# Seven half-size products for 16 up pairs, and the first FFN in blocks

## The chip, the cores and the metric

One core of a Trainium2 chip runs the program. The metric is device time in microseconds, the median of the runs. A core has TensorE (PE in the rows; PEld is its weight load), VectorE (DVE), ScalarE (ACT), GpSimd (POOL), and SyncE (SP), which only issues transfers here. Each engine works through its own queue in the order that was fixed when the program was built.

## The reference

A trunk of two layers over 512 positions with 1024 channels, float32. Each layer is a token mixer (gated linear attention, then a short gated convolution) and a causal ConvFFN, each behind an RMSNorm and with a residual addition; a last RMSNorm ends it. The change touches the first ConvFFN only:

```python
def conv_ffn(h, w_up, conv_w, w_down):
    up = causal_dwconv(h @ w_up, conv_w)      # depthwise, 3 taps over positions
    a, u = up[..., :D_FF], up[..., D_FF:]     # D_FF = 2816
    return (jax.nn.silu(a) * u) @ w_down
```

## The kernel before, in words

Activations stand transposed: `x[k]` is a tile of 128 channels by 512 positions, eight of them. Every float32 operand of a large product is split into a rounded part h and a rest l (both in the type fp32r), and a product is three matmuls, wh xh + wh xl + wl xh (`mm3`, L181). ScalarE makes h by a copy, VectorE makes l by a subtraction (L110, L111 for weights; L201, L202 for activations).

Weights come in units of 128 x 1024 (eight blocks of 128 x 128). `Weights.load` issues a unit's transfer on SP's queue into one of four raw tiles (`wraw`), `Weights.part` splits it into one of three pairs of tiles (`wsp`), and `Weights.take`, called before each group of matmuls, loads one unit further, splits the unit two ahead and gives out the current one. `group` (L188) takes a unit and runs its 24 matmuls of 512 columns into one of eight PSUM banks.

`ffn_up` (L487) runs over 22 pairs: the group of 128 gate channels, the group of 128 value channels; then the after-work: VectorE scales both by the inverse norm r (L499) into tiles u (three buffers), ScalarE and VectorE form the convolution (L245 to L247), ScalarE takes silu (L501), VectorE multiplies (L502), and the product is split into g{j}h and g{j}l (`split_to`). All 22 split products are held. Then the down stage: `residual` (L472) takes for each of eight blocks of channels one group of 66 matmuls over three units, adds it to x, and prepares the next norm (`norm_parts`, `norm_squares`).

The build has a planner that interleaves the queues: an instruction can stand before one that is earlier in the source when the planner finds it ready first; the silu, for example, stands ahead of the second convolution. The last row block of the second FFN is computed in two halves of 256 positions (`last_group`, L541), whose matmuls have 256 columns and a weight load each.

Of the kernel before, what the change touches and what calls it, by code (L numbers as in the profile page):

```python
# [10 lines left out]
F32 = mybir.dt.float32  # L11
F32R = mybir.dt.float32r
AF = mybir.ActivationFunctionType
ALU = mybir.AluOpType
# [14 lines left out]
DOWN_CUTS = ((0, 8), (8, 16), (16, 22))  # L29


@with_exitstack
def trunk_kernel(ctx, tc, xT, w_qk, w_v, w_g, w_up_gate, b_gate, w_go, w_sc, w_so, w_up, w_dn,
# [44 lines left out]
    class Weights:  # L78
        def __init__(self):
            self.units, self.raw, self.split, self.hold = [], {}, {}, {}  # L80
            self.nl = self.ns = self.ng = 0

        def load(self, between=lambda: None):
            if self.nl < len(self.units):
                src = self.units[self.nl]
                r = wraw.tile([P, UNIT], F32, tag="wraw", name=f"wr{self.nl}")
                n = src.shape[1]
                step = (UNIT // 4, UNIT // 2, UNIT)[min(self.nl, 2)]
                for c in range(0, n, step):
                    nc.sync.dma_start(r[:, c:min(c + step, n)], src[:, c:min(c + step, n)])  # L90
                    between()
                self.raw[self.nl] = r[:, :n]
                self.nl += 1

        def part(self):
            if self.ns < len(self.units):
                tiles = self.hold.pop(self.ns, lambda: None)()
                r = self.raw.pop(self.ns)
# [3 lines left out]
                if not tiles:  # L102
                    h = wsp.tile([P, UNIT], F32R, tag="wh", name=f"wh{self.ns}")
                    l = wsp.tile([P, UNIT], F32R, tag="wl", name=f"wl{self.ns}")
                blocks = []
                for i, c in enumerate(range(0, n, step)):
# [3 lines left out]
                    S.copy(hh, r[:, c:e])  # L110
                    V.tensor_sub(ll, r[:, c:e], hh.bitcast(F32))  # L111
# [4 lines left out]
        def take(self):  # L116

            self.load()
# [5 lines left out]
    W.units += [w_qk[i] for i in range(8)] + [w_v[i] for i in range(8)] + [w_g[i] for i in range(8)]  # L124
    W.units += [w_go[i] for i in range(8)]

    def ff_units(l):
        u = [w_up[l, j] for j in range(2 * NFF)]
        return u + [w_dn[l, m][:, a * P:b * P] for m in range(KD) for a, b in DOWN_CUTS]

    W.units += ff_units(0) + [w_sc[i] for i in range(3 * KD)] + [w_so[i] for i in range(KD)] + ff_units(1)
# [374 lines left out]
    gp = ffn_up(0)  # L506
    residual(lambda m: group(f"dn{m}", gp, nunits=3), 2)
# [31 lines left out]
    HT = T // 2  # L539
# [123 lines left out]
```

## Time and profile before

| | us |
|---|---|
| median of 3 runs (1117.83 to 1118.11) | 1117.9 |
| the profiled execution | 1117.47 |
| its span | 1115.8 |
| TensorE busy | 1106.3 |
| VectorE busy | 682.1 |
| ScalarE busy | 461.0 |
| POOL busy | 5.0 |

A busy share is a mean over stages with different limits. TensorE's matmuls overlap (each row's duration is longer than the step to the next), so a step is read from a stretch divided by its count, not from a mean duration. Transfers: 108.14 MB, 97 GB/s; nearly all on SP's queue, none issued by POOL.

### The profile page before, as it was taken

Reading aid. Unit: us, or ns where it says so; the run is one execution under the profiler, and the core shown is the slowest. Engines: PE = TensorE matmul, PEld = TensorE weight load, DVE = VectorE, ACT = ScalarE, POOL = GpSimd, SP = SyncE. Lnnn points to the kernel's source line nnn. Section 1 sums busy time; section 2 is a strip of 40 time slices with the busy share of each in tenths; the row PEclk is TensorE's granted clock in tenths of the full one; section 3 lists DMA queues with packets and bytes.
Section 4 is the critical chain, followed back from the end, with each engine's and each line's share of the span. In section 5 each row is a group of like instructions: output and inputs, shape, how many; then the busy total and the mean of one; then the engine's idle time right before and its main releaser. Section 6 shows DMA issues by size and latency. Waiting matters only on the chain.

```text
span 1115.8 us, 12505 instructions
## 1 busy us (share of the span) xinstructions
PE 1106.3 (99%) x5020; PEld 920.9 (83%) x5020; DVE 682.1 (61%) x854; ACT 461.0 (41%) x610; POOL 5.0 (0%) x18
## 2 busy tenths in 40 slices
PE   9999999999999999999999999999999999999997
PEld 7888888888888888888888888888888888888887
DVE  7864675597777777433336555558777777753232
ACT  6565664354444444332332222334444444432241
POOL 1000000000000000000000000000000000000000
PEclk9999999999999999999999999999999999999999
DMA  7231213222233222233232222222323222232312
GB/s 258 77 104 66 75 58 114 95 95 95 95 100 103 100 95 90 86 104 104 90 111 95 95 95 95 95 95 95 102 104 96 95 95 95 90 103 86 102 55 76
DMA packets 33182, 108.14 MB, mean 97 GB/s; under 512 B 3618, under 2 KB 6434, under 8 KB 33124
## 3 DMA queue, kind: packets, MB, share of 16 engines
q1 hardware_dynamic: 33124, 107.34, 29.5%
q8 instruction: 39, 0.64, 0.2%
q14 instruction: 19, 0.16, 0.0%
HBM read 105.23 MB, written 2.10 MB: 96 GB/s over the span
## 4 chain that ended last, share of the span: by engine, by line
PE 99%; DMA 0%; DVE 0%; ACT 0%; SPq 0%; issue 0%; DVEq 0%
PE up L186 43%; PE dn L186 20%; PE g L186 4%; PE v L186 4%; PE scb L186 4%; PE scu L186 4%; PE scc L186 4%; PE go L186 4%; PE so L186 4%; PE k L186 2%; PE q L186 2%; PE dn7b L186 1%; PE dn7a L186 1%; PE o L407 1%; PE o L409 0%; DMA x<-in_xT 0%
## 5 line engine op out<-in xcount | busy, mean ns | idle before, releaser
L110 ACT CAST wh<-wr 128x1024 fp32r<-128x1024 f32 (+3 forms) x201 | 204.8, 1019 | 370.8 <-PE dn L186 113.1
L111 DVE TENSOR_TENSOR wl<-wr,wh 128x1024 fp32r<-128x1024 f32 (+3 forms) x201 | 237.7, 1183 | 154.6 <-ACT wh L110 152.2
L186 PE MATMUL up<-xh,wh 128*128 128x512 f32 x704 | 273.9, 389 | 0.0
L186 PE MATMUL up<-xl,wh 128*128 128x512 f32 x704 | 273.9, 389 | 0.0
L186 PE MATMUL up<-xh,wl 128*128 128x512 f32 x704 | 273.9, 389 | 0.0
L186 PEld LDWEIGHTS up<-xl,wh 128*128 128x128 f32 x704 | 132.1, 188 | 27.6
L186 PEld LDWEIGHTS up<-xh,wh 128*128 128x128 f32 x704 | 132.1, 188 | 27.5
L186 PEld LDWEIGHTS up<-xh,wl 128*128 128x128 f32 x704 | 132.1, 188 | 27.2
L499 DVE TENSOR_TENSOR u<-up,r 128x512 f32<-128x512 f32 x88 | 60.2, 688 | 73.2 <-PE up L186 73.1
L247 DVE SCALAR_TENSOR_TENSOR c<-u,ffcw,c 128x510 f32<-128x510 f32 x88 | 65.7, 749 | 2.8
L246 DVE SCALAR_TENSOR_TENSOR c<-u,ffcw,c 128x511 f32<-128x511 f32 x88 | 65.3, 745 | 0.8 <-ACT c L245 0.8
L245 ACT ACTIVATE c<-u,ffcw 128x512 f32<-128x512 f32 x88 | 63.1, 721 | 2.8 <-DVE u L499 2.3
L501 ACT ACTIVATE c<-c 128x512 f32<-128x512 f32 x44 | 27.8, 632 | 81.7 <-DVE c L247 81.7
L502 DVE TENSOR_TENSOR c<-c,c 128x512 f32<-128x512 f32 x44 | 30.4, 692 | 1.6 <-ACT c L501 0.2
L239 DVE RECIPROCAL r<-r 128x512 f32<-128x512 f32 x8 | 26.8, 3353 | 4.7 <-ACT r L238 4.7
L222 ACT ACTIVATE sq<-x 128x512 f32<-128x512 f32 x34 | 21.0, 624 | 12.4 <-DVE x L536 10.7
L186 PE MATMUL g<-xh,wh 128*128 128x512 f32 x64 | 25.6, 400 | 0.0
L186 PE MATMUL v<-wh,xh 128*128 128x512 f32 x64 | 25.3, 395 | 0.0
L212 DVE SCALAR_TENSOR_TENSOR xl<-x,small,xh 128x512 fp32r<-128x512 f32 x32 | 23.7, 747 | 2.6 <-ACT xh L211 2.6
L186 PE MATMUL g<-xh,wl 128*128 128x512 f32 x64 | 25.0, 390 | 0.0
L186 PE MATMUL v<-wh,xl 128*128 128x512 f32 x64 | 24.9, 390 | 0.0
L186 PE MATMUL v<-wl,xh 128*128 128x512 f32 x64 | 24.9, 389 | 0.0
(798 smaller groups left out, 1859.0 us busy)
## 6 DMA issues: line engine op xcount, KB each, us to landing
wr<-in_w_up SPq DMA_DIRECT2D x88, 512.0 KB, 3.3
wr<-in_w_dn SPq DMA_DIRECT2D x32, 512.0 KB, 3.5
wr<-in_w_sc SPq DMA_DIRECT2D x24, 512.0 KB, 3.2
wr<-in_w_dn SPq DMA_DIRECT2D x16, 384.0 KB, 3.1
wr<-in_w_v SPq DMA_DIRECT2D x8, 512.0 KB, 3.3
wr<-in_w_g SPq DMA_DIRECT2D x8, 512.0 KB, 3.3
wr<-in_w_go SPq DMA_DIRECT2D x8, 512.0 KB, 3.3
wr<-in_w_so SPq DMA_DIRECT2D x8, 512.0 KB, 3.3
```

The costliest lines, as they stand in the source:

```text
L110: S.copy(hh, r[:, c:e])
L111: V.tensor_sub(ll, r[:, c:e], hh.bitcast(F32))
L186: PE.matmul(out, lhsT=a, rhs=b, start=first and i == 0, stop=last and i == 2)
L212: V.scalar_tensor_tensor(l, x[k], col(gi, k), h.bitcast(F32), op0=ALU.mult, op1=ALU.subtract)
L222: S.activation(sq, x[k], AF.Square)
L239: V.reciprocal(r, r)
L245: S.activation(c, u, AF.Copy, scale=cw[:, 2:3])
L246: V.scalar_tensor_tensor(c[:, 1:], u[:, :T - 1], cw[:, 1:2], c[:, 1:], op0=ALU.mult, op1=ALU.add)
L247: V.scalar_tensor_tensor(c[:, 2:], u[:, :T - 2], cw[:, 0:1], c[:, 2:], op0=ALU.mult, op1=ALU.add)
L499: V.tensor_mul(u, ups[i], r)
L501: S.activation(cs[0], cs[0], AF.Silu)
L502: V.tensor_mul(cs[1], cs[1], cs[0])
```

## The change

The first FFN no longer runs all 22 pairs and then all down groups. It runs in four blocks of 6, 5, 5 and 6 pairs (`BLOCKS`, `ff_steps`): the eight down groups of a block stand between the pairs of the next block, one or two behind each pair, the last block's at the end. A down group has 18 or 15 matmuls, and its result is added to x each time, so x gets four additions in place of one. The split products of two blocks share tiles (`b{j % 11}`).

Pairs 6 to 21 (`SEVEN`) are computed as a 2 x 2 block product: two blocks of output channels (gate, value), two halves of the 1024 inner channels, two halves of the 512 positions. In place of eight products of half size there are seven (Strassen, in Winograd's form), each of 4 blocks x 3 terms of 256 columns (`product`). Their operands are sums:

- of weights, four of 128 x 512 for each pair. GpSimd issues them as transfers that add to their destination: in `sums` behind the load, the value unit's second half onto its first half, and the gate unit's first half onto a second copy of the value unit's first half, which SP loads a second time; in `forms` the value sum onto the gate unit's first half, and that onto the gate unit's second half, each once the split of the old contents is done. A pair's weights are split in four units (`forms`, q = 0 to 3) of 1024, 1024, 1024 and 512 columns.
- of activations, made once after pairs 1 to 4 by `seven_forms` on ScalarE and VectorE and kept split.
- of results: bank A takes four products on top of each other, bank C two, B one (`up_seven`). ScalarE copies A out after the first, second and third product and C after its first; VectorE forms three differences and sums of these, ScalarE copies the fourth.

`take` can now load two units at once (both of a pair), and loads only when the raw tile's last split is already in the queue.

```diff
--- before.py
+++ after.py
@@ -27,6 +27,8 @@
 UNIT = 1024
 WARM = 10
 DOWN_CUTS = ((0, 8), (8, 16), (16, 22))
+BLOCKS = ((0, 6), (6, 11), (11, 16), (16, 22))
+SEVEN = range(6, 22)
 
 
 @with_exitstack
@@ -76,13 +78,32 @@
 
 
     class Weights:
+
+
+
         def __init__(self):
-            self.units, self.raw, self.split, self.hold = [], {}, {}, {}
+            self.units, self.srcs, self.need, self.last = [], [], [], []
+            self.raw, self.split, self.hold = {}, {}, {}
+            self.paired, self.third, self.npair = set(), {}, 0
             self.nl = self.ns = self.ng = 0
 
+        def add(self, src):
+            self.srcs.append(src)
+            self.last.append(len(self.units))
+            self.need.append(len(self.srcs) - 1)
+            self.units.append(None)
+
+        def add_pair(self, a, b):
+            n, i = len(self.srcs), len(self.units)
+            self.srcs += [a, b]
+            self.paired.add(n + 1)
+            self.last += [i + 3, i + 2]
+            self.need += [n + 1] * 4
+            self.units += [(n, q) for q in range(4)]
+
         def load(self, between=lambda: None):
-            if self.nl < len(self.units):
-                src = self.units[self.nl]
+            if self.nl < len(self.srcs):
+                src = self.srcs[self.nl]
                 r = wraw.tile([P, UNIT], F32, tag="wraw", name=f"wr{self.nl}")
                 n = src.shape[1]
                 step = (UNIT // 4, UNIT // 2, UNIT)[min(self.nl, 2)]
@@ -91,44 +112,109 @@
                     between()
                 self.raw[self.nl] = r[:, :n]
                 self.nl += 1
+                if self.nl - 1 in self.paired:
+                    self.sums(self.nl - 2)
+
+        def halve(self, hh, ll, src):
+            S.copy(hh, src)
+            V.tensor_sub(ll, src, hh.bitcast(F32))
+
+        def sums(self, n):
+
+            ra, rb = self.raw[n], self.raw[n + 1]
+            lo, hi = slice(0, T), slice(T, 2 * T)
+            s = bt(f"b13{'hl'[self.npair % 2]}", f"s{n}")
+            self.npair += 1
+            nc.sync.dma_start(s, self.srcs[n + 1][:, lo])
+            G.dma_start(rb[:, lo], rb[:, hi], accum_op=ALU.add)
+            G.dma_start(s, ra[:, lo], accum_op=ALU.add)
+            self.third[n] = s
+
+        def forms(self, n, q, h, l):
+
+
+            ra, rb = self.raw[n], self.raw[n + 1]
+            lo, hi = slice(0, T), slice(T, 2 * T)
+            if q == 0:
+                self.halve(h[:, lo], l[:, lo], ra[:, lo])
+                G.dma_start(ra[:, lo], rb[:, lo], accum_op=ALU.add)
+                self.halve(h[:, hi], l[:, hi], self.third.pop(n))
+            elif q == 1:
+                self.halve(h[:, hi], l[:, hi], ra[:, hi])
+                G.dma_start(ra[:, hi], ra[:, lo], accum_op=ALU.add)
+                self.halve(h[:, lo], l[:, lo], ra[:, lo])
+            elif q == 2:
+                self.halve(h, l, rb)
+            else:
+                self.halve(h[:, lo], l[:, lo], ra[:, hi])
 
         def part(self):
             if self.ns < len(self.units):
+                while self.nl <= self.need[self.ns]:
+                    self.load()
                 tiles = self.hold.pop(self.ns, lambda: None)()
-                r = self.raw.pop(self.ns)
+                pair = self.units[self.ns]
+                if not tiles:
+                    h = wsp.tile([P, UNIT], F32R, tag="wh", name=f"wh{self.ns}")
+                    l = wsp.tile([P, UNIT], F32R, tag="wl", name=f"wl{self.ns}")
+                if pair:
+                    self.forms(pair[0], pair[1], h, l)
+                    self.split[self.ns] = (h, l)
+                    self.ns += 1
+                    return
+                r = self.raw.pop(self.need[self.ns])
                 n = r.shape[1]
                 whole = 8 <= self.ns < 16
                 step = UNIT // 2 if tiles else (UNIT // 4, UNIT // 2, UNIT)[min(self.ns, 2)]
-                if not tiles:
-                    h = wsp.tile([P, UNIT], F32R, tag="wh", name=f"wh{self.ns}")
-                    l = wsp.tile([P, UNIT], F32R, tag="wl", name=f"wl{self.ns}")
                 blocks = []
                 for i, c in enumerate(range(0, n, step)):
                     e = min(c + step, n)
                     hh, ll = tiles[i] if tiles else (h[:, c:e], l[:, c:e])
                     hh, ll = hh[:, :e - c], ll[:, :e - c]
-                    S.copy(hh, r[:, c:e])
-                    V.tensor_sub(ll, r[:, c:e], hh.bitcast(F32))
+                    self.halve(hh, ll, r[:, c:e])
                     blocks += [(hh[:, b:b + P], ll[:, b:b + P]) for b in range(0, e - c, P)]
                 self.split[self.ns] = (h, l) if whole else blocks
                 self.ns += 1
 
         def take(self):
 
-            self.load()
+            for _ in range(2):
+                if self.nl < len(self.srcs) and (self.nl < 4 or self.last[self.nl - 4] < self.ns):
+                    self.load()
+                    if self.nl not in self.paired:
+                        break
             self.part()
             self.ng += 1
             return self.split.pop(self.ng - 1)
 
     W = Weights()
-    W.units += [w_qk[i] for i in range(8)] + [w_v[i] for i in range(8)] + [w_g[i] for i in range(8)]
-    W.units += [w_go[i] for i in range(8)]
-
-    def ff_units(l):
-        u = [w_up[l, j] for j in range(2 * NFF)]
-        return u + [w_dn[l, m][:, a * P:b * P] for m in range(KD) for a, b in DOWN_CUTS]
-
-    W.units += ff_units(0) + [w_sc[i] for i in range(3 * KD)] + [w_so[i] for i in range(KD)] + ff_units(1)
+    for src in ([w_qk[i] for i in range(8)] + [w_v[i] for i in range(8)] + [w_g[i] for i in range(8)]
+                + [w_go[i] for i in range(8)]):
+        W.add(src)
+
+
+    def ff_steps():
+        steps = [("up", j) for j in range(*BLOCKS[0])]
+        for b in range(1, len(BLOCKS)):
+            n = BLOCKS[b][1] - BLOCKS[b][0]
+            for i, j in enumerate(range(*BLOCKS[b])):
+                steps.append(("up", j))
+                steps += [("dn", b - 1, m) for m in range(KD * i // n, KD * (i + 1) // n)]
+        return steps + [("dn", len(BLOCKS) - 1, m) for m in range(KD)]
+
+    for st in ff_steps():
+        if st[0] == "dn":
+            a, b = BLOCKS[st[1]]
+            W.add(w_dn[0, st[2]][:, a * P:b * P])
+        elif st[1] in SEVEN:
+            W.add_pair(w_up[0, 2 * st[1]], w_up[0, 2 * st[1] + 1])
+        else:
+            W.add(w_up[0, 2 * st[1]])
+            W.add(w_up[0, 2 * st[1] + 1])
+    for src in ([w_sc[i] for i in range(3 * KD)] + [w_so[i] for i in range(KD)]
+                + [w_up[1, j] for j in range(2 * NFF)]
+                + [w_dn[1, m][:, a * P:b * P] for m in range(KD) for a, b in DOWN_CUTS]):
+        W.add(src)
     take = W.take
 
 
@@ -503,8 +589,102 @@
             gp.append(split_to(cs[1], f"g{j}", f"b{j}"))
         return gp
 
-    gp = ffn_up(0)
-    residual(lambda m: group(f"dn{m}", gp, nunits=3), 2)
+    def seven_forms(k, gi, y):
+
+
+        lo, hi = slice(0, HT), slice(HT, T)
+        g1, g2 = col(gi, k), col(gi, k + 4)
+        S.activation(y[:, lo], x[k][:, hi], AF.Copy, scale=g1)
+        S.activation(y[:, hi], x[k + 4][:, hi], AF.Copy, scale=g2)
+        ta, tb = wk("ta", tag="sq"), wk("tb", tag="sq")
+        V.scalar_tensor_tensor(ta[:, lo], x[k][:, lo], g1, y[:, lo], op0=ALU.mult, op1=ALU.subtract)
+        V.tensor_sub(tb[:, lo], y[:, lo], y[:, hi])
+        V.scalar_tensor_tensor(ta[:, hi], x[k][:, lo], neg[:, k:k + 1], tb[:, lo], op0=ALU.mult, op1=ALU.add)
+        V.scalar_tensor_tensor(tb[:, hi], x[k + 4][:, lo], g2, ta[:, hi], op0=ALU.mult, op1=ALU.add)
+        a = split_to(ta, f"ta{k}", f"b{14 + 2 * k}")
+        b = split_to(tb, f"tb{k}", f"b{15 + 2 * k}")
+        return [tuple(p[:, c] for p in t) for t in (a, b) for c in (lo, hi)]
+
+    def product(out, ws, xs, first):
+        for k in range(4):
+            c = slice(k * P, (k + 1) * P)
+            wh, wl = ws[0][:, c], ws[1][:, c]
+            for i, (a, b) in enumerate(((wh, xs[k][0]), (wh, xs[k][1]), (wl, xs[k][0]))):
+                PE.matmul(out, lhsT=a, rhs=b, start=first and k == 0 and i == 0, stop=k == 3 and i == 2,
+                          skip_group_check=not first)
+
+    def up_seven(j, tf):
+
+        lo, hi = slice(0, HT), slice(HT, T)
+        cut = lambda ks, c: [tuple(p[:, c] for p in xparts[k]) for k in ks]
+        b11, b21, b22 = cut(range(4), lo), cut(range(4, 8), lo), cut(range(4, 8), hi)
+        t1, t2, t3, t4 = tf
+        half = lambda w, c: (w[0][:, c * T:(c + 1) * T], w[1][:, c * T:(c + 1) * T])
+        n = "hl"[j % 2]
+        sa, sb = bt(f"b11{n}", "sa"), bt(f"b12{n}", "sb")
+        A, C = ps("upa")[:, 0:HT], ps("upc")[:, 0:HT]
+        w = take()
+        product(A, half(w, 0), b11, True)
+        S.copy(sa[:, lo], A)
+        product(C, half(w, 1), t3, True)
+        S.copy(sa[:, hi], C)
+        w = take()
+        product(A, half(w, 0), t2, False)
+        S.copy(sb[:, lo], A)
+        B = ps("upb")[:, 0:HT]
+        product(B, half(w, 1), b21, True)
+        w = take()
+        product(A, half(w, 0), t1, False)
+        S.copy(sb[:, hi], A)
+        product(C, half(w, 1), t4, False)
+        w = take()
+        product(A, half(w, 0), b22, False)
+        us = [wk("u", bufs=3) for _ in range(2)]
+        V.tensor_add(us[0][:, lo], sa[:, lo], B)
+        V.tensor_sub(us[1][:, lo], C, sb[:, lo])
+        V.tensor_sub(us[1][:, hi], sa[:, hi], sb[:, hi])
+        S.copy(us[0][:, hi], A)
+        return us
+
+    def ffn_blocks(l, gi, gnext):
+        gp, r, tf = {}, None, [[], [], [], []]
+        V.tensor_scalar_mul(neg, vec[:, gi * KD:(gi + 1) * KD], -1.0)
+        for st in ff_steps():
+            if st[0] == "dn":
+                _, b, m = st
+                part = group(f"dn{m}", [gp[j] for j in range(*BLOCKS[b])])
+                V.tensor_add(x[m], x[m], part)
+                if b == len(BLOCKS) - 1:
+                    norm_parts(m, gnext)
+                    norm_squares(m)
+                continue
+            j = st[1]
+            if j in SEVEN:
+                us = up_seven(j, tf)
+                for u in us:
+                    V.tensor_mul(u, u, r)
+            else:
+                ups = [group("up0", xparts)]
+                if j == 0:
+                    sums = sum_parts(acc[0])
+                ups.append(group("up1", xparts))
+                if j == 0:
+                    r = inv_rms_rows(sums, D)
+                    y = wk("y", tag="acc", bufs=1)
+                us = [wk("u", bufs=3) for _ in range(2)]
+                for u, up in zip(us, ups):
+                    V.tensor_mul(u, up, r)
+            cs = [conv3(us[i], ffcw[:, l, i * NFF + j, :], f"c{i}") for i in range(2)]
+            S.activation(cs[0], cs[0], AF.Silu)
+            V.tensor_mul(cs[1], cs[1], cs[0])
+            gp[j] = split_to(cs[1], f"g{j}", f"b{j % 11}")
+            if len(SEVEN) and 1 <= j <= 4:
+                for t, f in zip(tf, seven_forms(j - 1, gi, y)):
+                    t.append(f)
+
+    HT = T // 2
+    neg = tk("neg", (P, KD), bufs=1)
+    ffn_blocks(0, 1, 2)
 
 
     yparts = []
@@ -536,7 +716,6 @@
         V.tensor_add(x[m], x[m], group(f"dn{m}", gp, nunits=3))
         norm_squares(m)
     wlast = take() + take() + take()
-    HT = T // 2
 
     def last_group(op, th, ks):
         c = slice(th * HT, (th + 1) * HT)
```

## Rows read from the trace of the kernel before

**Rows 1.** The page: busy us (share) xinstructions; 40 slices in tenths, and the granted clock.

```profile
PE 1106.3 (99%) x5020; PEld 920.9 (83%) x5020; DVE 682.1 (61%) x854; ACT 461.0 (41%) x610; POOL 5.0 (0%) x18
...
PE   9999999999999999999999999999999999999997
...
PEclk9999999999999999999999999999999999999999
```

**Rows 2.** The chain that ended last, in order of time: start us, us, what.

```profile
222.11 228.48 PE up L186 x1008
450.59 119.68 PE dn L186 x528
...
1089.34 7.91 PE dn7a L186 x66
```

**Rows 3.** Stretches: length, busy of PE, PEld, DVE, ACT, POOL, PEclk, DMA share, GB/s.

```profile
222.11:450.59 228.48, 228.48 (x1009) 189.19 (x1009) 171.12 (x214) 102.55 (x132) 0.00 (x0) 1.00 0.29 96
227.95:241.70 13.75, 13.75 (x63) 11.37 (x62) 13.57 (x19) 8.65 (x12) 0.00 (x0) 1.00 0.21 62
...
0.00:27.90 27.90, 25.98 (x103) 20.51 (x104) 20.15 (x34) 19.45 (x33) 3.96 (x16) 1.00 0.75 258
```

**Rows 4.** VectorE by line and shape: busy us, mean ns | idle before.

```profile
L111 DVE TENSOR_TENSOR wl<-wr,wh 128x1024 fp32r<-128x1024 f32 x180 | 220.4, 1224 | 153.7 <-ACT wh L110 151.3
L247 DVE SCALAR_TENSOR_TENSOR c<-u,ffcw,c 128x510 f32<-128x510 f32 x88 | 65.7, 749 | 2.8
L246 DVE SCALAR_TENSOR_TENSOR c<-u,ffcw,c 128x511 f32<-128x511 f32 x88 | 65.3, 745 | 0.8 <-ACT c L245 0.8
L499 DVE TENSOR_TENSOR u<-up,r 128x512 f32<-128x512 f32 x88 | 60.2, 688 | 73.2 <-PE up L186 73.1
...
L111 DVE TENSOR_TENSOR wl<-wr,wh 128x768 fp32r<-128x768 f32 x15 | 14.4, 959 | 0.2 <-ACT wh L110 0.2
...
L536 DVE TENSOR_TENSOR x<-x,dn 128x512 f32<-128x512 f32 x7 | 4.8, 687 | 21.9 <-PE dn L186 21.9
...
L111 DVE TENSOR_TENSOR wl<-wr,wh 128x512 fp32r<-128x512 f32 x2 | 1.3, 688 | 0.3 <-ACT wh L110 0.3
```

**Rows 5.** ScalarE by line and shape, the same columns.

```profile
L110 ACT CAST wh<-wr 128x1024 fp32r<-128x1024 f32 x180 | 189.5, 1053 | 332.3 <-issue 82.7 <-PE dn L186 77.1 <-PE up L186 58.4
L245 ACT ACTIVATE c<-u,ffcw 128x512 f32<-128x512 f32 x88 | 63.1, 721 | 2.8 <-DVE u L499 2.3
L501 ACT ACTIVATE c<-c 128x512 f32<-128x512 f32 x44 | 27.8, 632 | 81.7 <-DVE c L247 81.7
...
L396 ACT ACTIVATE sta<-kva,wst 128x256 f32<-128x256 f32 x4 | 1.9, 464 | 0.0
...
L110 ACT CAST wh<-wr 128x512 fp32r<-128x512 f32 x2 | 1.1, 610 | 0.0
```

**Rows 6.** TensorE and VectorE at a group's end, and TensorE behind VectorE: start, us.

```profile
7.47 0.76 DVE xl L212
8.27 0.73 PE q L186 x2
...
1097.09 0.28 PE L186 MATMUL dn7b<-g0h,wlast00h 128*128 128x256 f32 x1
...
1097.29 0.42 DVE L549 TENSOR_TENSOR x<-x,dn7a 128x256 f32<-128x256 f32 x1 [5.83 <-PE dn7a L186]
```

**Rows 7.** Transfers: issuing queue, count, KB each, us from issue to landing.

```profile
wr<-in_w_up SPq DMA_DIRECT2D x88, 512.0 KB, 3.3
...
out<-o SPq DMA_DIRECT2D x8, 256.0 KB, 2.3
...
zraw<-in_w_up_gate SPq DMA_DIRECT2D x4, 32.0 KB, 5.8
```

## The prediction

> **What bounds the kernel now.** I read the page's busy shares and slices first: the reader is to see TensorE busy 1106.3 us of a span of 1115.8, every slice but the last at 9 or more, and the granted clock at full speed throughout, which is the 2.4 GHz level [rows 1]. Then the chain of waits in order of time: the first FFN's up stage is one piece of 228.48 us and 1008 matmuls, its down stage one piece of 119.68 us and 528, with no other engine between [rows 2]. So TensorE sets the end, and a matmul of 512 columns costs 228.48/1008 = 0.2267 us. The change swaps these for matmuls of 256 columns with a weight load each. The trace has such a stretch: 66 in 7.91 us, 0.1198 us each [rows 2]. That is more than half of 0.2267, by 6.5 ns, so half-size products lose some of what they save in columns.
>
> The stretches say what room the other engines have. Over the up stage VectorE is busy 171.12 of 228.48 us (75%), ScalarE 102.55 (45%), the DMA engines 0.29 at 96 GB/s [rows 3].
>
> **The change part by part.** TensorE, one pair: before 2 groups x 8 blocks x 3 terms = 48 matmuls, 48 x 0.2267 = 10.88 us. After, 7 products x 4 blocks x 3 terms = 84 of 256 columns, 84 x 0.1198 = 10.06 us. The gain is 0.81 us a pair, **13.0 us over 16 pairs** (1.2%, although the columns fall by an eighth). Six pairs stay as they were. The down stage keeps 528 matmuls, only cut in four groups a row block. If the end stays on TensorE without gaps, 13.0 us is all of it; the edit can win no more, since nothing else is removed from TensorE.
>
> VectorE, one pair before: two subtractions of 1024 columns at 1.224, two scalings u at 0.688, the convolution 2 x (0.745 + 0.749), the product and the split at 0.69 each: 8.2 us, which agrees with 171.12/21 [rows 3, 4]. After: the weights have seven halves in place of four, as five subtractions of 512 (0.688) and one of 1024, 4.66; three recombinations of 256 columns at 0.42 [rows 6], 1.26; the scalings, convolution, product and split as before, 5.75. Sum **11.7 us against 10.06 of TensorE**. VectorE would be the bound in a pair alone. What covers it are the down units put behind each pair: one of 18 matmuls is 18 x 0.2267 = 4.08 us of TensorE, one of 15 is 3.40, and costs VectorE only its split (0.96 for 768 columns, between 0.69 and 0.96 for 640, I take 0.83) and one addition to x at 0.687: 1.65 or 1.52 [rows 4]. From ff_steps: a stretch from one pair to the next has one or two such units. Counted over the 15 stretches between 16 pairs: 2 with one unit of 18, 3 with two of 18, 6 with one of 15, 4 with two of 15. TensorE and VectorE then have:
> one of 15: 13.46 and 13.2 us (98%); one of 18: 14.14 and 13.35 (94%); two of 15: 16.86 and 14.7 (87%); two of 18: 18.22 and 15.0 (82%).
> So on eight stretches VectorE is all but full. That is possible: in 227.95 to 241.70 it was busy 13.57 of 13.75 us and TensorE did not pause, because the results wait in PSUM [rows 3]. But that stretch had weights split ahead. Here the split of a pair's second unit stands in the queue behind the whole after-work of the pair before it. Placing it: its buffer is free when TensorE has done the fourth unit (10.06 after the pair's start), the after-work fills VectorE from 8.8 to about 17, with gaps of 0.7 where it waits for ScalarE's silu (0.632) and cast (0.61) [rows 5]; two subtractions of 0.69 in these gaps end at about 17.1, wanted at 13.46 + 2.88 = 16.34. Bounds: 0 (the order is kinder) to 0.8 us a stretch. I take 0.5 on eight stretches with one unit: **4.0 us back**. The long stretches have 3.4 us more and lose none.
>
> PSUM reuse. Bank A takes four products in turn, C two; before each but the first, ScalarE must have copied the half sum out, and a matmul waits for it. The cover is the one product between, 12 x 0.1198 = 1.44 us. Three of the waits a pair are this short, 48 in all. The copy: a reader started 0.20 us after the next group's first matmul [rows 6], 256 columns out of PSUM cost ScalarE 0.464 [rows 5], and TensorE starts about 0.04 after an engine's end (8.27 against 7.47 + 0.76) [rows 6]: 0.70, so 0.74 us is spare. ScalarE is busy 9.9 of 13.46 us by the same counting (five casts of 512, one of 1024, five copies of 256, two convolution scalings at 0.721, silu, the split's cast, the unit's cast), and what it does when A falls due lasts at most 1.053 (the 1024 cast): 0 to 0.3 us a wait, or more where two stand ahead. I take 0.05: **2.4 us back**.
>
> The sums of the weights. Four transfers of 256 KB a pair on POOL's queue, 64 in all, and 16 loads of 256 KB more on SP's. No adding transfer stands in the trace, nor any issue from POOL. Bounds by the nearest rows: a plain 256 KB transfer lands after 2.3 us, a queued one after 5.8; as an add reads two operands, it moves what a 512 KB load reads, 3.3 [rows 7]. I take 3.3 for one, a. The Trainium skill (DMA: Bandwidth & Descriptors, Anatomy of one DMA) fits a POOL-issued transfer as 2.0 us plus bytes over 436e3; that is an estimate of 2.6 us here, no run here shows it, and the sum below stays the same by it. Two adds follow each other before the second unit (rb, then ra low), behind a load whose slot is freed late. From a pair's start: the last unit's buffer is free at 2.88, cast and subtraction end at 2.88 + 0.61 + 0.69 + waits = 4.3, which frees the slot; load 3.3; two adds 2a; cast and subtraction 1.3; then TensorE's second unit, 2.88 into the next pair. So a stretch with one unit cannot be shorter than 4.3 + 3.3 + 2a + 1.3 - 2.88 = 6.0 + 2a; with two units both loads wait for that slot, and 2.0 (512 KB at 258 GB/s, the densest stretch [rows 3]) comes on top, 8.0 + 2a. At 3.3 these are 12.6 and 14.6, under 13.46 and 16.86: hidden, with 0.86 us of cover. ScalarE's queue stands behind such a late cast, its PSUM copies too. Bandwidth: a short stretch moves 1.6 MB of loads and four adds of 0.5 MB, 3.6 MB in 13.46 us, 270 GB/s, where 258 made the engines 0.75 busy [rows 3]; so a may well be above 3.3.
>
> The input forms: pairs 1 to 4 get four operations of 256 and two subtractions of 512 more, 1.7 + 1.4 = 3.1 us, 11.3 of VectorE against 10.88; 1.7 us of lag in all, behind the reciprocal at pair 0, and PSUM's eight banks took the lag of 227.95 to 241.70, which such a reciprocal had left [rows 3]: I take nothing, bounds 0 to 1.7. The 24 further additions to x (24 x 0.69 = 16.5 us) are counted above. The last pair's after-work ends before the last block needs it: two units and 14 matmuls, some 10 us.
>
> **Sum.** The profiled execution took 1117.47 us, span 1115.8, 1.7 around it; the median of the runs is 0.4 higher. 1117.5 - 13.0 + 4.0 + 2.4 = 1110.9: **1111 us**.
>
> **Rivals.**
> Full gain: the queue's order puts the late split first and ScalarE is free in time: 1117.5 - 13.0 = 1104.5. For it: the 13.57 of 13.75 us. Against: eight stretches at 94 to 98%.
> Nothing gained: VectorE's after-work and the copies out of A take 0.81 us a pair; with a copy one cast too late (0.27 us a wait, 48 waits = 13.0) or with 0.8 on eight stretches and 0.14 a wait. 1117.5. For it: both take only a queue order one instruction worse than I placed.
> Slower: the chain of load, add, add is the bound of the stretches. It decides from a = 4.6: 6.0 + 9.2 = 15.2, 1.74 x 6 + 1.06 x 2 + 0.34 x 4 = 13.9. At a = 5: 2.54 x 6 + 1.86 x 2 + 1.14 x 4 = 23.5, so 1117.5 - 13.0 + 23.5 = **1128**; at the queued row's 5.8: 4.14 x 6 + 3.46 x 2 + 2.74 x 4 + 1.38 x 3 = 46.9, so 1151. For it: 270 GB/s, and three kinds of transfer meeting. Against: 3.3 for a load of the same bytes.
> POOL held off by VectorE: if each issue had to wait for VectorE's running instruction, at most 1.22, a would be 4.5, the stretches 15.0 and 17.0: 1.54 x 6 + 0.86 x 2 + 0.14 x 4 = 11.5, so with the 2.4 1118.4. The Trainium skill (SBUF — State Buffer, SBUF: two separate sides) has this rule, for VectorE operations that use both ports, as a copy within SBUF. The rows speak against it: 512 columns take 0.688 and 1024 take 1.224, 1.05 ns a column, and of the changed stage's operations with one tensor only a reciprocal and a change of sign of 8 columns stand on VectorE [rows 4].
>
> **How the numbers follow.** Forecast 0.40 (1106 to 1115), full gain 0.14, nothing gained 0.14, POOL held off 0.02, slower 0.30. A measurement here tells 0.2% (2.2 us) from no change: faster 0.54, same 0.16, slower 0.30. The range leaves out some 0.05 below and 0.15 above: 1103 to 1131.
>
> **What would show it.** TensorE: products of 12 matmuls at 0.120 us, gaps at the second unit of a pair released by VectorE (my 4.0) and before products on A released by ScalarE (my 2.4). If the gaps are released by a DMA, or casts of ra low wait for one, it is the chain; the adds' time to landing, under 3.7 or over 4.6 us, decides. VectorE over 90% in the three blocks; without that my counting is wrong. If the 256-column matmuls take over 10.88/84 = 0.1295 us, the change loses on TensorE itself.

## The result and the profile after

The changed kernel takes 1151.46 us (median; 1146.32 to 1152.42), the kernel before beside it on the same chip 1117.87: ratio 1.0292, 95% interval [1.0276, 1.0307]. It is slower by 3%; I had said 1111, 1103 to 1131. The profiled execution took 1152.35 us, its span is 1150.3.

The page after, answering to [rows 1]: busy us, shares and counts, the slices, the granted clock, and the chain that ended last by engine.

```profile
PE 1107.2 (96%) x5596; PEld 947.5 (82%) x5596; DVE 752.0 (65%) x1023; ACT 519.3 (45%) x778; POOL 60.4 (5%) x82
...
PE   9999999999899988897999999999999999999997
...
PEclk9999999999999999999999999999999999999999
...
PE 78%; DMA 13%; ACT 3%; DVE 3%; issue 2%; SPq 0%; POOL 0%; POOLq 0%; DVEq 0%; ACTq 0%
```

TensorE's share falls from 99% to 96%, and the slices show where: from the eleventh to the nineteenth, the stage of the pairs. The chain now has 13% of DMA in it. VectorE, which I had feared, is at 65%, and at 70% (200.13 of 285.34 us) in the stage of the pairs.

Stretches after, with the columns of [rows 3]: the whole first FFN, the 15 stretches between 16 pairs, 3 us behind one wait, and 3 us behind another.

```profile
211.15:604.80 393.65, 360.65 (x2163) 324.60 (x2163) 289.14 (x437) 198.93 (x345) 55.39 (x64) 0.97 0.56 140
280.00:565.34 285.34, 252.59 (x1675) 234.84 (x1676) 200.13 (x311) 138.24 (x257) 50.94 (x59) 0.96 0.64 153
449.00:452.00 3.00, 3.00 (x17) 3.00 (x17) 0.70 (x2) 1.26 (x3) 0.00 (x0) 0.54 0.59 186
374.46:377.46 3.00, 3.00 (x25) 3.00 (x26) 1.97 (x3) 1.17 (x3) 0.00 (x0) 1.00 0.56 106
```

Before, the first FFN ran from 210.78 to 570.27, 359.49 us. Less my 13.0 it would be 346.5; it is 393.65, 47.2 more. Of these 33.0 are TensorE's idle time (393.65 - 360.65) and 14.2 are in its busy time (360.65 - 346.5). Most of the 14.2 is the clock, and the third row shows how. TensorE had stood idle for 3.55 us until 447.74; from 449 to 452 the granted clock was 0.54, close to the level of 1.2 GHz, and 17 matmuls of 256 columns took 3.00 us, 0.176 each in place of 0.120. Before, the clock stood at full speed throughout the first FFN. Not every wait did this: behind one of 2.06 us that ended at 374.46 the clock stayed at 1.00 (fourth row), and 25 matmuls fitted into 3.00 us. Of the 16 waits six, of 2.06 to 3.74 us (a second one of 2.06 among them), were followed by a stretch at 0.50, of 20.5 us together, which cost half of that, 10.2 us. The other 4 us lie at the edges of the waits: the row of the last matmul before a wait runs 0.16 us beyond its step and counts as busy, and the first matmul behind it takes 0.22 us to the next in place of 0.12, so 0.26 a wait. 1117.5 - 13.0 + 33.0 + 14.2 = 1151.7 against 1152.35 of the profiled execution, so hardly anything changed outside the first FFN.

Who waited for whom after: engine, what, line, released by what: us in total, times, longest.

```profile
PE upa L613 <- ACT sa L628: 33.0, 16, 3.7
...
ACT wh L119 <- DMA wr<-wr: 75.4, 29, 5.3
...
POOL wr L144 <- DMA wr<-wr: 45.3, 14, 4.7
```

All of TensorE's idle time is one wait a pair, at the second unit: bank A must have been copied out by ScalarE. But the copy takes under 0.4 us (0.28 of it in the chain below); ScalarE stands in front of it, in a cast that waits for an adding transfer. The chain after shows what that transfer waited for, in order of time from one pair's second add to the next pair's second unit (start us, us, what):

```profile
348.25 3.20 DMA wr<-wr
...
351.99 3.18 DMA wr<-wr
...
355.24 0.63 ACT wh L119
...
355.90 0.70 DVE wl L120
...
356.61 4.71 DMA wr<-in_w_up
...
361.39 0.49 issue
361.88 6.42 DMA wr<-wr
...
368.37 0.47 issue
...
368.85 3.18 DMA wr<-wr
...
373.19 0.95 ACT wh L119
374.14 0.28 ACT sa L628
...
374.46 1.69 PE upa L613 x12
376.16 1.44 PE upb L613 x12
```

Second add, third add, cast and subtraction, which free a raw tile; load, first add, second add of the next pair; casts, copy, TensorE. Between 348.25 and 373 the chain holds nothing of TensorE. The same pair's second unit had started at 353.89, so this stretch, a long one with two down units of 18 matmuls, took 20.6 us where TensorE's own work was 18.2 by my count.

The stretches don't all end in this chain. In at least three of the eight short ones (those with one down unit), the one from 280.33 among them, it runs through TensorE:

```profile
284.90 1.33 PE upc L613 x11
...
286.30 1.15 ACT wh L119 x2
287.46 0.69 DVE wl L120
...
288.48 5.02 DMA wr<-wr
```

TensorE frees a split buffer, the next pair's first unit is cast and subtracted, and only then may the second add overwrite the gate unit's low half, which that unit was split from. The second unit started at 295.93, 15.6 us behind the one before. This wait of the second add for the first unit's split isn't in my prediction.

The transfers after, the columns of [rows 7]:

```profile
wr<-in_w_up SPq DMA_DIRECT2D x88, 512.0 KB, 3.5
wr<-wr POOLq DMA_DIRECT2D x48, 256.0 KB, 3.4
s<-in_w_up SPq DMA_DIRECT2D x16, 256.0 KB, 2.6
```

The median of the adds is near my 3.3. By kind it is 4.5 for the first add (3.4 to 7.3), 4.1 for the one onto s (3.2 to 6.3), 3.3 and 3.2 for the second and third, and each behind another transfer is preceded by about 0.5 us of issue in the chain. Medians of 3.2 to 4.5 lie on both sides of the signs that I had set (under 3.7, over 4.6), so these did not decide. The long ones had company: during the first add at 361.88, issued 0.11 us before a load, the DMA engines moved 191 GB/s, during the third add at 351.99 they moved 88 GB/s, little more than its own 256 KB. No run takes the loads away to show this by itself.

Each experiment below is also read by its stretches: from the first matmul of one pair's second unit to that of the next. Eight of the 15 hold one down unit, seven hold two. The changed kernel's take 16.7 us (15.4 to 17.5) and 20.4 us (19.8 to 21.3) in the mean, together 276.1.

### The profile page after: what moved, and what is told of

Same layout as the page of the kernel before. It is cut to its first block, busy times and chain, and to the rows that moved or that the text cites. A ratio compares the mean times of both kernels' runs of the same rounds, so it can differ in the third digit from the quotient of the medians.

```text
span 1150.3 us, 14295 instructions
## 1 busy us (share of the span) xinstructions
PE 1107.2 (96%) x5596; PEld 947.5 (82%) x5596; DVE 752.0 (65%) x1023; ACT 519.3 (45%) x778; POOL 60.4 (5%) x82
## 4 chain that ended last, share of the span: by engine, by line
PE 78%; DMA 13%; ACT 3%; DVE 3%; issue 2%; SPq 0%; POOL 0%; POOLq 0%; DVEq 0%; ACTq 0%
PE up L272 26%; PE dn L272 13%; DMA wr<-wr 9%; PE g L272 4%; PE v L272 4%; PE so L272 4%; PE scb L272 4%; PE scc L272 4%; PE scu L272 4%; PE go L272 4%; PE upa L613 3%; ACT wh L119 2%; DMA wr<-in_w_up 2%; PE k L272 2%; PE q L272 2%
## 5 line engine op out<-in xcount | busy, mean ns | idle before, releaser
L119 ACT CAST wh<-wr 128x1024 fp32r<-128x1024 f32 (+4 forms) x257 | 227.5, 890 | 386.9 <-DMA wr<-wr 75.4
L120 DVE TENSOR_TENSOR wl<-wr,wh 128x1024 fp32r<-128x1024 f32 (+4 forms) x257 | 263.0, 1024 | 134.6 <-ACT wh L119 133.2
L272 PE MATMUL up<-xh,wh 128*128 128x512 f32 x448 | 174.3, 389 | 0.0
L272 PE MATMUL up<-xl,wh 128*128 128x512 f32 x448 | 174.3, 389 | 0.0
L272 PE MATMUL up<-xh,wl 128*128 128x512 f32 x448 | 174.3, 389 | 0.0
L272 PEld LDWEIGHTS up<-xh,wh 128*128 128x128 f32 x448 | 84.1, 188 | 17.6
L272 PEld LDWEIGHTS up<-xh,wl 128*128 128x128 f32 x448 | 84.1, 188 | 17.5
L272 PEld LDWEIGHTS up<-xl,wh 128*128 128x128 f32 x448 | 84.1, 188 | 17.3
L613 PE MATMUL upa<-xh,wl 128*128 128x256 f32 x128 | 36.2, 283 | 0.0
L613 PE MATMUL upa<-xl,wh 128*128 128x256 f32 x128 | 36.2, 283 | 0.0
```

Source lines behind the costliest of these rows:

```text
L119: S.copy(hh, src)
L120: V.tensor_sub(ll, src, hh.bitcast(F32))
L272: PE.matmul(out, lhsT=a, rhs=b, start=first and i == 0, stop=last and i == 2)
L613: PE.matmul(out, lhsT=a, rhs=b, start=first and k == 0 and i == 0, stop=k == 3 and i == 2, skip_group_check=not first)
```

## Experiments

The theory (A): the load, the adds in series and the casts that free a raw tile form a loop that is longer than TensorE's work. Rivals: VectorE's or ScalarE's work on the products; GpSimd held off; TensorE closing the loop; a cost of each adding transfer wherever it stands (D).

**Blocks alone (e1).** `SEVEN = range(0)`: the first FFN by blocks, every pair by ordinary products.

> The four blocks and the four-part down groups alone, no pair by seven products. Every theory but one: TensorE has the same 48 matmuls a pair and 528 in the down stage, so 1117.9 within 2.2 us. If the blocks themselves (24 more additions to x on VectorE, smaller down groups) cost something, 1120 to 1130, with TensorE waiting in the first FFN.

Measured 1117.47 us, ratio 0.9999 [0.9989, 1.0008]. The 24 further additions to x and the other order cost nothing, as priced.

**No sums (e2).** The four adding transfers are left out.

```
-            G.dma_start(rb[:, lo], rb[:, hi], accum_op=ALU.add)
-            G.dma_start(s, ra[:, lo], accum_op=ALU.add)
...
-                G.dma_start(ra[:, lo], rb[:, lo], accum_op=ALU.add)
...
-                G.dma_start(ra[:, hi], ra[:, lo], accum_op=ALU.add)
```

> All four adding transfers of a pair left out (the weights' sums are then missing from the result); products, splits, copies and loads stay. Theory A, the loop of transfers over the raw tiles is the bound: TensorE takes over, 1104.5 to 1111, idle of TensorE in the first FFN under 7 us instead of 33.0, clock 1.00. Theory B, VectorE's and ScalarE's queues (my forecast's terms, larger than sized): their work is unchanged, so 1135 or more, the idle before the second unit stays above 20 us. Theory C, the half-size products themselves: 1150.

Measured 1106.04 us, ratio 0.9897 [0.9882, 0.9911]. The window over the same 15 stretches:

```profile
279.38:511.12 231.74, 231.74 (x1616) 217.62 (x1615) 191.71 (x301) 137.19 (x247) 0.00 (x0) 1.00 0.37 116
```

TensorE never waits, and 231.74 us is what my counting of the 15 stretches gave (6 x 13.46 + 2 x 14.14 + 4 x 16.86 + 3 x 18.22 = 231.1). VectorE is at 83%. So everything but the sums behaves, B and C fall, and the sums hold 45 us.

**No third add (e3).** The last of the four lines alone is left out.

> Only the third adding transfer of the chain left out (gate unit's first half onto its second; that sum is missing from the result). Theory A with the loop closed through the raw tile, that is add to ra low, add to ra high, cast and subtraction, slot, load, add to rb, add to ra low: without one add of 3.2 and its issue of 0.5 the loop falls from some 17.4 to 13.7 us on stretches with one down unit, at TensorE's 13.5 to 14.1: 1108 to 1120. If the loop closes through TensorE instead, as my prediction had it (two adds in series), leaving out this add changes nothing on the path: 1145 to 1152. Theory B: 1145 to 1152.

Measured 1146.89 us, ratio 1.0248 [1.0215, 1.0281]: 4.6 us back, not 30 to 40. The theory as it then stood, a loop through the third add alone, fell; the time lies in the range that I had given for a loop closed through TensorE (1145 to 1152). The chain of this kernel, up to one second unit:

```profile
406.74 1.15 DVE wl L120
...
407.90 3.41 DMA wr<-in_w_up
...
411.87 3.47 DMA wr<-wr
...
416.64 4.83 DMA wr<-wr
...
422.03 1.04 ACT wh L119
...
423.91 1.70 PE upa L612 x12
```

In this stretch, without the third add, the value unit's tile closes the loop: subtraction of 1024, load, first add, second add, casts. From the load's landing (411.31) to that of the second add (421.47) is 10.2 us.

**Sums on GpSimd (e4).** The same four sums as `G.tensor_add` in place of the transfers.

> The four sums made by GpSimd as elementwise additions of 512 columns, in place of transfers; the result is the reference's. Theory A: if one takes under 2 us, the loop falls from 17.4 to about 11 us, under TensorE's share: 1105 to 1113. Rival: GpSimd's additions hold up VectorE's operations with two inputs (or are held up by them); at four additions of 1 to 1.5 us a pair VectorE's 13.2 us on a short stretch become 17 to 19: 1140 to 1165, and VectorE's rows for 512 columns come out longer than 0.69 us.

Measured 1143.59 us, ratio 1.0235 [1.022, 1.025]. GpSimd's and VectorE's operations by line and shape (columns as in [rows 4]):

```profile
L140 POOL TENSOR_TENSOR wr<-wr,wr 128x512 f32<-128x512 f32 x16 | 30.4, 1897 | 38.5 <-DVE wl L120 18.4 <-issue 15.2 <-ACT g4h L287 4.9
...
L665 DVE TENSOR_TENSOR u<-u,r 128x512 f32<-128x512 f32 x32 | 35.8, 1119 | 0.6
...
L645 DVE TENSOR_TENSOR u<-sa,sb 128x256 f32<-128x256 f32 x16 | 9.1, 566 | 4.7 <-ACT sb L638 4.2
...
L644 DVE TENSOR_TENSOR u<-upc,sb 128x256 f32<-128x256 f32 x16 | 6.8, 425 | 7.2 <-PE upc L613 7.2
```

The time lies in the rival's range. An add is shorter than a transfer (1.53 to 1.90 us in the mean, by line), but several of VectorE's operations with two operands in SBUF take longer in the mean: u<-u,r 1119 ns in place of 688, u<-sa,sb 566 in place of 425. The operation of the same 256 columns with one operand in PSUM, u<-upc,sb, kept its 425. The Trainium skill (SBUF — State Buffer, Who interferes with whom) says that a VectorE instruction with two SBUF inputs contends with a GpSimd instruction that reads SBUF; these rows agree.

**The second add twice (e5).** Line 140 is issued two times (its sum is then another).

> The second adding transfer (value sum onto the gate unit's first half) issued twice, one behind the other; the result then has a wrong sum. Theory A, as it stands after the run without the third add: the loop is second add, casts of the second and third unit on ScalarE with the subtraction behind, the value unit's raw tile free, load, first add, second add. One more add in it costs its 3.2 us and 0.5 of issue on each of 15 stretches: 1195 to 1215. Rival D, the transfers slow everything by their load on the DMA engines, in no particular chain: a fourth more of what the four cost (45 us): 1158 to 1168.

Measured 1198.55 us, ratio 1.0722 [1.0701, 1.0744]: 47 us more. The stretches take 19.6 and 23.3 us, 2.9 more each, nearly what one add and its issue take: the second add lies in the chain of every stretch, and D's 1158 to 1168 fell.

**Five raw tiles (e7).** `bufs=4` to `bufs=5` for the raw tiles, and `take` may load into the fifth. The tile takes 4 KB a partition; to make room, a table moved into another tile and small tiles were merged.

> Five raw tiles in place of four (the causal mask of the attention moves into a tile that is free then, to make room). Theory A: behind one down unit the next value unit no longer waits for a tile of its own pair, so the loop is open on the eight short stretches (3 us each and part of the slow clock); the long ones keep it: 1115 to 1130. Rival D: the same transfers: 1145 to 1155.

Measured 1127.52 us, ratio 1.0086 [1.0069, 1.0103]; stretches 15.5 and 18.5. A load that starts a tile earlier gives back 24 us, so a loop is closed in the raw tiles: closed through TensorE alone it would not have moved. The time is in A's range, but the long stretches gave more each (1.9) than the short ones (1.2), the other way round than I expected: the short ones come down to about the length of the chain through TensorE (15.6 above).

**Value unit first (e8).** The pair is loaded in the other order, and the first add goes out with its load.

```
-            self.srcs += [a, b]
+            self.srcs += [b, a]
...
```

> The value unit loaded ahead of the gate unit, its first add and the second copy issued with it; the same transfers, the same result. Theory A: the first add leaves the loop, because the value unit then takes the raw tile that is free earlier; what stays is tile free, load of the gate unit, its split, second add, some 12 us on short stretches and 14.5 on long ones, under TensorE's 13.5 and 16.9: 1105 to 1114. Rival D: 1145 to 1155.

Measured 1148.75 us, ratio 1.028 [1.0262, 1.0297]: a miss, 35 us above what I expected and in D's range. GpSimd's instructions in order of time (start, us, line, what, idle before and its end):

```profile
417.14 0.86 POOL L118 DMA_DIRECT2D s<-wr  x1 [5.61 <-DMA wr<-in_w_up]
423.44 0.86 POOL L141 DMA_DIRECT2D wr<-wr  x1 [5.45 <-issue]
427.72 0.86 POOL L145 DMA_DIRECT2D wr<-wr  x1 [3.42 <-DMA wr<-wr]
```

I had overlooked a wait. The add onto s (417.14) reads the gate unit's low half; the second add (423.44) overwrites it and must let that read end: it landed at 422.93, and the second add went out 0.51 us later. So two adds still stood in series behind a load, only others.

**Both (e9).** Five raw tiles and the swap.

> Both: five raw tiles and the value unit first. Theory A: TensorE is the bound, no better than the value unit first by more than 3 us: 1104 to 1111. Rival D: 1145 to 1155.

Measured 1124.52 us, ratio 1.0062 [1.0047, 1.0077]; stretches 15.5 and 18.1. Far under D, and a miss for A by 13 us; the value unit first gave 3 us here.

**Value unit first, and s summed from device memory (e10).** The wait just found goes:

```
-                    G.dma_start(self.third[self.nl - 2], r[:, 0:T], accum_op=ALU.add)
...
+            G.dma_start(s, self.srcs[n + 1][:, lo], accum_op=ALU.add)
```

> The swap of e8 (value unit loaded first), and the sum s now adds the gate unit's half straight from device memory, so that it no longer reads the gate unit's raw tile and the second add needs to wait for it no more. Four raw tiles as in the changed kernel. Theory A (two transfers in series between the load of one raw tile and the casts that free it): one add leaves the loop; it is then gate tile free, load 3.5, subtraction of its low half 1.3, issue 0.5, second add 3.3, casts of the second and third unit and the subtraction 3.1, together 11.7 us and so under TensorE's 13.5 to 14.1 us of the short stretches: 1105 to 1114, TensorE's wait for the copy sa under 10 us in all. Rival D (whatever the order, the transfers of the queue that adds share something, so their number counts and not their order): as e8, 1144 to 1152.

Measured 1126.07 us, ratio 1.0068 [1.0051, 1.0085]: 22.7 less than with the swap alone at the same 64 adds, so D falls; but 12 above A's range. The seven long stretches are nearly TensorE's own now (18.1; 17.5 without sums), the short ones 15.2 where TensorE alone has 13.7. The chain over such a stretch:

```profile
455.25 1.33 PE upc L613 x11
...
456.61 1.15 ACT wh L119 x2
...
457.80 0.69 DVE wl L120
...
458.78 4.91 DMA wr<-wr
...
464.24 1.04 ACT wh L119
...
465.81 0.27 ACT sa L628
```

The loop is another, the one through TensorE, which some short stretches of the changed kernel already end in: TensorE frees a split buffer, the first unit is cast and subtracted, the second add may then overwrite its source, casts, copy, TensorE.

**The same with five raw tiles (e11).**

> e10 with five raw tiles. Theory A: the loads start a tile earlier, no loop is left that is longer than TensorE's work: 1105 to 1111. Rival D: no better than the same with five tiles and s summed out of the raw tile, 1122 to 1127.

Measured 1127.65 us, ratio 1.0081 [1.0065, 1.0097]; stretches 15.4 and 18.0. A miss too, and it fits the loop just shown: more raw tiles don't help where TensorE closes it.

**Every second pair (e12).** The changed kernel with `SEVEN = range(7, 22, 2)`, 8 pairs.

> The changed kernel with every second pair only by seven products (8 pairs, j = 7, 9, ... 21), so 32 adds fewer and a pair of ordinary products between any two that need adds. Theory A: the loop of 16 to 17 us now has the 14 us of the ordinary pair beside it as well, so no wait is left: the gain is 8 times 0.81 = 6.5 us, less 1 to 2 us for the forms of x and the late splits: 1112 to 1114. Rival E (each pair with adds costs TensorE its 2 to 3 us wherever it stands, since the chain load-add-add starts only when its pair is at hand): 1117.9 + 8 * 2.1 = about 1134.

Measured 1111.54 us, ratio 0.9944 [0.9926, 0.9962], a little under A's range: no wait of TensorE in the stage is left. With an ordinary pair between, the loop fits, and 6.35 of 6.5 us of gain arrive.

**The third add twice (e13).** Line 144 is issued two times (another sum).

> The changed kernel with the third add (high half of the gate unit's tile) issued twice instead of the second: the same 16 extra transfers of 256 KB on the same queue as in e5, and like it the output is not the reference's. Theory A: the third add isn't in the loop of the short stretches (the value unit's tile comes free without it), only its own slack of about two units of TensorE's work goes: 1152 to 1175. Rival D (each adding transfer costs its 3 us wherever it stands): as e5, 1195 or more.

Measured 1196.17 us, ratio 1.0702 [1.0674, 1.0729]: as much as the second add twice, a miss for A by over 20 us and what D had said. Its chain:

```profile
388.75 3.58 DMA wr<-wr
...
392.86 3.19 DMA wr<-wr
...
396.33 5.59 DMA wr<-wr
...
402.47 0.38 ACT sb L634
402.89 2.38 PE upa L614 x12
```

The cast of the fourth unit waits for the third add, and on ScalarE the next copies stand behind it. I read it so: two chains of nearly one length stood side by side, one through the value unit's tile (load, first, second add), one through the gate unit's (second, third add, cast, load). Lengthening either costs its full price, taking one away (the third add) nearly nothing. No run shows this reading by itself; that D, which fits here and with the value unit first, is not the cause stands on the five raw tiles and on the sum from device memory, which kept all 64 adds and gave 24 and 25 us back.

**Two of three pairs (e14)**, in the order of e11.

> e11 (value unit first, s summed from device memory, five raw tiles) with two of every three pairs by seven products: 11 of them, after every two an ordinary pair. Theory A: only the second pair of two meets the loop, and the ordinary pair gives the loads 14 us to catch up: 11 times 0.81 = 8.9 us gained, at most 5 waits of about 1 us and the forms' 1 us against it: 1109 to 1113. Rival E (each pair with adds costs its wait wherever it stands): e11 lost 1127.7 - 1104.5 = 23 us on 16 pairs, so 11 pairs 16 us: 1117.9 - 8.9 + 16 = 1125.

Measured 1112.65 us, ratio 0.9956 [0.9939, 0.9972], as A expected.

**The second sum in a tile of its own (e15).** e10, where the second add goes onto another copy of the gate unit's low half, so that it waits for no split:

```
+            nc.sync.dma_start(t, self.srcs[n + 1][:, lo])
...
-                G.dma_start(ra[:, lo], rb[:, lo], accum_op=ALU.add)
+                G.dma_start(self.second[n], rb[:, lo], accum_op=ALU.add)
```

> e10 with four raw tiles, where the second sum has a tile of its own: the low half of the gate unit is loaded there once more (256 KB) and the second add goes onto that, so it overwrites nothing that the first unit's split still has to read. Theory A with the loop through TensorE (buffer freed by TensorE, split of the first unit, second add, splits, copy out of bank A: 15.4 us): that loop loses the add, the stretches with one unit go to 14.0 to 14.6: 1107 to 1115. Rival F (the load of the value unit, first add and second add, 12 us and the waits between, hold the short stretches whoever overwrites what): as e10, 1122 to 1128.

Measured 1118.4 us, ratio 1.0000 [0.9984, 1.0015]. The trace was taken in a second run of the same kernel (e17):

> e15 once more, for a trace at full clock: 1114 to 1120. By the loop through TensorE the stretches with one unit are now under 15.3 us; by rival F they end in a chain of the value unit's load, first add and second add.

Measured 1116.56 us, ratio 0.9985 [0.9967, 1.0002]. TensorE's wait in it:

```profile
PE upa L618 <- ACT sa L633: 9.4, 10, 2.2
```

The short stretches fell to 14.4 (13.6 to 15.2), below e10's 15.2, so the loop through TensorE was there; the long ones rose from 18.1 to 18.4 with one transfer more a pair. The time lies between what A and F expected. What is left, some 10 us over e2, was not taken apart.

**The same with two of three pairs (e16).**

> The same with two of every three pairs by seven products (11). With the loop through TensorE: no wait left, 1117.9 - 8.9 + 1.5 = 1110, 1108 to 1111. Rival F: as e14, 1112 to 1113.

Measured 1110.2 us, ratio 0.9932 [0.9916, 0.9949]. Its page:

```profile
PE 1098.3 (99%) x5416; PEld 933.1 (84%) x5416; DVE 736.9 (67%) x988; ACT 505.5 (46%) x733; POOL 43.1 (4%) x62
```

It is faster than both kernels, than the one before by 0.7%: 11 pairs keep 7.4 of their 8.9 us.

## Why the prediction was wrong

The step that failed is **the sums of the weights**, at "I take 3.3 for one, a" and the "hidden" that followed. The loop was named, and its formula for a stretch, 6.0 + 2a and 8.0 + 2a, stood there; its terms were too small, a above all. The long stretch whose chain is shown took 20.6 us where the formula gave 8.0 + 2 x 3.3 = 14.6. Its two adds take from 361.32 (the load's landing) to 372.03, 10.7 us in place of 6.6, so 5.35 each: 0.5 of issue before each, and a first add of 6.42. I compared an add with a plain load's landing of 3.3 and left out the issue, and I took one value for a loop in which the adds meet other transfers. My 270 GB/s didn't come either: an add counts as 256 KB, and the 15 stretches moved 153 GB/s. The fit from the Trainium skill (DMA: Bandwidth & Descriptors, Anatomy of one DMA), 2.6 us, was further off: no add landed in under 3.1.

The ends of the loop were off as well. I let TensorE free the buffer 4.3 us after a pair's start, 1.4 after its second unit's (4.3 - 2.88). In that chain it is the third add, by way of a cast, that releases the tile, 2.7 us after the second unit's start (356.60 against 353.89), and from the second add's landing to the next second unit it takes 2.4 us in place of 1.3; the load's 4.7 are within the 5.3 that I had for two.

And a wait was left out: the second add must let the first unit's split end, and so waits for TensorE. At least three of the eight short stretches of the changed kernel end in that chain, with one add in it (15.6 us in the one shown), and so do most of e10's (15.2 in the mean). So the short stretches' 16.7 us equal 6.0 + 2 x 5.35 by chance: for the long ones the same a gives 18.7, and they took 20.4.

The rival with a = 5.8 gave 1151, which is the time that came. Its mechanism, adds in series as the bound, was right: two stand in the chain of ten of the 15 stretches (in seven the first and the second, in three the one onto s and the second). Its number is partly luck. It put 46.9 us on the waits alone, where 33.0 came as idle time and 14.2 in the busy time, and it held neither the clock nor the wait for the split.

The other steps, one by one. Half-size products: 12 matmuls of 256 in 1.44 us, 0.120 each, as taken; of the gain of 13.0, 12.5 show in the first FFN without adds (e2: 347.0 us in place of 359.5). VectorE's cover: predicted at 82 to 98% by stretch, 209.7 us over all 15, measured 191.7 without adds (e2), 83%. The durations were counted rightly, they add up to 209.2 us there; but rows that follow each other directly overlap (in the changed kernel one of 0.68 us starts at 381.58, the next at 382.19), so VectorE is less full than a sum of durations says. Late splits and copies out of bank A, 4.0 + 2.4: nothing, as TensorE has no idle time in e2's first FFN. Blocks: nothing, as taken (e1). GpSimd held off by VectorE: no sign of it in the changed kernel, whose adds go through transfers (the issue of every second add took 0.86 us); with adds on GpSimd it appeared, from VectorE's side (e4). The clock's fall behind a wait: not priced at all.

## What to carry to other kernels

Price a transfer in a loop by what its chain takes with issue and neighbours, not by the landing of the nearest plain load, and write the loop out with every wait in it, those for reads by other transfers too; a forecast that rests on 0.86 us of cover in a loop of unmeasured parts deserves the rival's chance. Where such a loop is longer than the work beside it, the change can still be used less often: with an ordinary pair between, the loop had room and nearly all of the gain arrived. An idle TensorE can cost more than its idle time; read the granted clock behind each wait. And a sum of durations is an upper bound of an engine's busy time where its rows overlap.

## What the runs showed of the hardware

A transfer of 256 KB that adds within SBUF landed after 3.1 to 7.4 us, and its issue mostly held GpSimd for 0.86 us; one that adds from device memory landed after 4.1 to 6.2 us (e10). Adds of 512 columns on GpSimd took 1.53 to 1.90 us in the mean, and VectorE's product of 512 columns beside them 1.12 us in the mean in place of 0.69, while its 256 columns with one operand in PSUM stayed at 0.425. After an idle time of 2.63 us TensorE's granted clock over the next 3.15 us was 0.65, and after one of 3.55 us it was 0.54 from 1.3 to 4.3 us behind it; after one of 2.06 us it stayed at 1.00 over the next 3.00 us, and after another of 2.06 us it fell to 0.50.
